# Head outputs of the first branch: transposed by VectorE in 32x32 blocks before they go to DRAM, instead of by TensorE after they come back

## The chip, the cores and the metric

One core of one Trainium2 chip runs the whole kernel. The metric is device time in microseconds of one execution. All times below are from the profile (one execution, with a start and an end for each instruction) or from separate timed runs.

An engine takes its own instructions in order. TensorE is PE in the profile (PEld is its weight load), VectorE is DVE, ScalarE is ACT, GpSimd is POOL, and SyncE is SP. SP issues nearly all transfers on one queue, also in order: an issue that waits for a buffer or for data holds back all issues behind it.

## The reference

The reference is one layer of a hybrid network on 512 tokens of width 1024, in float32: a feed-forward block, a mixing block, a second feed-forward block. The change lies in the mixing block:

```python
z = u @ w_mix + b_mix
q_m, k_m, v_m, o_m, i_m, f_m, q_f, k_f, v_f, f_f, g_a, g_b = split(z)
q_m, k_m = split(silu(causal_conv(concat(q_m, k_m))))
h_m = mlstm_chunkwise(q_m, k_m, v_m, i_m, f_m)            # 4 heads, 256 values each
y_a = sigmoid(o_m) * rms_norm(h_m, mlstm_norm_g).reshape(B, S, 1024)
y_b = forgetting_attention(q_f, k_f, v_f, f_f, ...)       # 16 heads of 64
merged = sigmoid(g_a) * (y_a @ w_branch_a) + sigmoid(g_b) * (y_b @ w_branch_b)
x = x + g2 * (merged @ w_out)
```

`h_m` is the output of the first branch's four heads. It is normalised over each head's 256 values, multiplied by a gate `sigmoid(o_m)`, and then multiplied by `w_branch_a`.

## The kernel before

**Tiling.** 128 partitions (P); the 512 tokens are four blocks of 128 (NT = 4), the width is eight blocks of 128. Each float32 matmul is three passes over parts of the operands: high by high, high by low, low by high (`mm3`, L125 to L129). A weight tile `raw` is loaded by SP, its high part `wh` is made by ScalarE (L102) and its low part `wl` by VectorE (L104). Results go to PSUM banks of two pools: four g banks for the large products, four t banks for the rest. One bank is 128x512.

**The mixing block in order of time.** After the products for the first branch's queries, keys and values (`v_mlstm` makes the values of two heads at a time: bias added by L1037 into `vf`, then `vm` by L1041 and L1042), each of the four heads runs `mlstm_w` (the weights `W`, made from `Mb`, a row of DRAM broadcast to 128 partitions, L1056 to L1078) and `mlstm_h` (the head's output). Between and after these come the second branch's 16 heads: `fox_qkv` (products and normalisation), `fox_s` and `fox_p` (scores, softmax), `fox_o`. The products that do not depend on a head, such as `gate` (tanh of a product into `tg`, then to DRAM as `g_d`) and `y_a`, are generators, and their matmuls are used to fill PE between the heads' steps. The eight `y_a` run between 745 and 820 us, the heads of the first branch end between 480 and 555 us.

**mlstm_h.** Tokens lie on partitions: for each of the four token blocks, matmuls `t<-vm,Wh` give a bank of 128x256 (and two columns for the denominator); L1094 to L1098 divide and write `hn`, one half of a tile of 128x2x256 of tag bc. L1100 sums the squares over the 256 columns (ScalarE). L1103 and `rsqrt` (L146 to L154) make the factors of all four blocks at once, L1106 scales each block in place, and L1107 stores each block (128x256, 128 KB) in a DRAM tensor `h_d` of 512x1024.

**y_a.** Here features lie on partitions, since `y_a` is the moving operand of a later product. For feature block m, eight groups of three matmuls (`gemm_stat`) give `o_m` of 128 features by 512 tokens, L1302 loads the 128 columns of `h_d` as a tile `ht` of 128x4x128 (256 KB, rows of 512 bytes), and four PE transposes (L1305, a matmul with the identity each) put them in a t bank. ScalarE copies the bank into `ya` with a factor (L1307), VectorE multiplies with the gate (L1308).

**What sets the order.** The code is run through a framework that allocates tiles from pools and orders the instructions of each engine itself from program order and its own estimates. A tile has a tag and a tag has a fixed number of buffers; a new tile of the tag waits until the last reader of the oldest is done, and for a tile that is stored this means until the store has landed. The tags that matter: t2 (3 buffers: `hj`, `vf`, `tg`, `th`, `fj`, `vg`, `yt`; `self.tmp` takes one), bc (4 buffers: `hn`, `Mb`, `Mm`, `A`, `Am`), tok (4 buffers: `ht` and token tiles of the second branch).

Of the kernel before, what the change touches and what calls it, by code (L numbers as in the profile page):

```python
# [11 lines left out]
F32 = mybir.dt.float32  # L12
F32R = mybir.dt.float32r
I32 = mybir.dt.int32
AF = mybir.ActivationFunctionType
# [5 lines left out]
P = 128  # L21
T = 512
NT = 4
# [24 lines left out]
class Layer:  # L48
# [1032 lines left out]
    def mlstm_h(self, h, ip):  # L1081
        nc, sp = self.nc, self.sp
        (Wh, Wl), (vh, vl) = self.W[h], self.vt[h]
        ss = sp.tile([P, NT], F32, name=self.nm("hs"), tag="hs", bufs=2)
        hs = []
        for tb in range(NT):
            if tb % 2 == 0:
                h2 = ip.tile([P, 2, 256], F32, name=self.nm("hn"), tag="bc", bufs=4)
            ps = self.tbank()
            for sb in range(tb + 1):  # L1090
                o = W_OFF[sb] + (tb - sb) * P
                self.mm3(ps[:, :258], Wh[:, o:o + P], Wl[:, o:o + P], vh[:, sb, :], vl[:, sb, :], sb == 0, sb == tb)
            d = sp.tile([P, 1], F32, name=self.nm("d"), tag="d", bufs=4)
            nc.vector.tensor_scalar(d, ps[:, 256:257], -1.0, self.gcol[:, tb, 32 + h:33 + h], op0=MUL, op1=MAX)  # L1094
            nc.vector.tensor_tensor(d, d, ps[:, 256:257], op=MAX)
            nc.vector.reciprocal(d, d)
            hn = h2[:, tb % 2, :]
            nc.vector.tensor_scalar(hn, ps[:, 0:256], d, None, op0=MUL)  # L1098
            j = ip.tile([P, 256], F32, name=self.nm("hj"), tag="t2", bufs=3)
            nc.scalar.activation(j, hn, AF.Square, accum_out=ss[:, tb:tb + 1])  # L1100
            hs.append(hn)
        v = sp.tile([P, NT], F32, name=self.nm("hv"), tag="hv", bufs=2)
        nc.vector.tensor_scalar(v, ss, 1.0 / 256, EPS, op0=MUL, op1=ADD)  # L1103
        r = self.rsqrt(v, NT)
        for tb in range(NT):
            nc.vector.tensor_scalar(hs[tb], hs[tb], r[:, tb:tb + 1], None, op0=MUL)  # L1106
            nc.sync.dma_start(self.h_d[tb * P:(tb + 1) * P, h * 256:(h + 1) * 256], hs[tb])  # L1107


    def fox_qkv(self, g, ip):  # L1110
# [176 lines left out]
    def y_a(self, m, ap, ip):  # L1287
        nc = self.nc
        def step():
            if m >= NK // 2:  # L1290
                self.tick()
                next(self.ada)
        ps = self.gbank()
        w = self.w_stat(self.A["w_mix"][0], OM + m * P)
        self.gemm_stat(ps, w, 0, T, range(0, 4))
        step()
        yield
        self.gemm_stat(ps, w, 0, T, range(4, 8))
        th = self.tmp(ip, "th")
        nc.scalar.activation(th, ps, AF.Tanh, scale=0.5, bias=self.hom[:, m:m + 1])  # L1300
        ht = ip.tile([P, NT, P], F32, name=self.nm("ht"), tag="tok", bufs=4)
        nc.sync.dma_start(ht, self.h_d[:, m * P:(m + 1) * P].rearrange("(b p) n -> p b n", p=P))  # L1302
        b = self.tbank()
        for tb in range(NT):
            nc.tensor.transpose(b[:, tb * P:(tb + 1) * P], ht[:, tb, :], self.ident)  # L1305
        ya = ap.tile([P, T], F32, name=self.nm("ya"), tag="qk", bufs=16)
        nc.scalar.activation(ya, b, AF.Copy, scale=self.hmg[:, m:m + 1])  # L1307
        nc.vector.scalar_tensor_tensor(ya, th, 1.0, ya, op0=ADD, op1=MUL)  # L1308
        self.ya[m] = ya
        step()  # L1310
        yield
# [347 lines left out]
```

## Time and profile before

| | us |
|---|---|
| runs, median (lowest to highest of 3) | 1319.72 (1318.76 to 1320.57) |
| profiled execution, its own time | 1320.06 |
| its span (first to last instruction) | 1318.2 |
| PE busy | 1303.2 |
| DVE busy | 955.4 |
| ACT busy | 629.6 |

The span is the time between the first and the last instruction in the trace; the execution's own time has some start and end around it. A row of the timeline gives start, length, engine, line, operation, output and inputs, count, and in brackets the engine's idle time before it and what ended it. Where several equal instructions follow each other, one row shows them with their count, and the length is that of the group. Numbers behind a tile's name are left out in the profile and kept in rows of the order of instructions.

### The profile page before, as it was taken

The numbers are of one execution on the slowest core, as the hardware profiler recorded it, in microseconds if no ns is written. First come the engines' busy times: TensorE is split into PE (matmuls) and PEld (weight loads), VectorE is DVE, ScalarE is ACT, GpSimd is POOL, SyncE is SP. The second block draws the span as 40 slices with busy tenths as digits, with TensorE's granted clock in tenths as the row PEclk, the third lists the DMA queues.
The fourth block names the chain that finished last, engine by engine and source line by source line (L and its number), as shares of the span: only waits on it lengthen the run. The fifth ranks groups of instructions, "written<-read, shape, count | busy, mean of one in ns | idle before, by whom it ended". The sixth has DMA issues, their size and how long they took to land.

```text
span 1318.2 us, 17786 instructions
## 1 busy us (share of the span) xinstructions
PE 1303.2 (99%) x6341; PEld 1092.7 (83%) x6341; DVE 955.4 (72%) x1736; ACT 629.6 (48%) x1054; POOL 36.9 (3%) x57
## 2 busy tenths in 40 slices
PE   7999999999999999999999999999999999999998
PEld 6788888888899888888888888888898888888887
DVE  6887767478688687887887778777567556635787
ACT  5533232355476555566666666334372223223651
POOL 1000000000010101000000000003000000000000
PEclk9999999999999999999999999999999999999999
DMA  9899978465845334533342536777539777634574
GB/s 294 262 326 303 320 268 281 136 193 163 301 126 145 106 111 129 160 104 109 88 129 73 167 105 190 219 251 237 184 104 327 248 238 279 219 100 136 171 263 149
DMA packets 204488, 254.18 MB, mean 193 GB/s; under 512 B 15008, under 2 KB 146752, under 8 KB 204400
## 3 DMA queue, kind: packets, MB, share of 16 engines
q1 hardware_dynamic: 204016, 252.98, 60.4%
q8 instruction: 50, 0.82, 0.3%
q14 instruction: 38, 0.31, 0.1%
q0 software_dynamic: 320, 0.06, 0.0%
q10 hardware_dynamic: 64, 0.02, 0.0%
HBM read 217.28 MB, written 35.72 MB: 192 GB/s over the span
## 4 chain that ended last, share of the span: by engine, by line
PE 93%; DVE 3%; ACT 2%; DMA 1%; issue 1%; ACTq 0%; DVEq 0%
PE g L129 23%; PE g L127 23%; PE g L128 23%; PE t L127 4%; PE t L129 4%; PE t L128 4%; PE g L897 2%; PE t L1280 1%; PE t L1250 1%; PE t L1221 1%; PE t L897 1%; PE t L1222 1%; PE t L797 1%; ACT uh L263 0%; DVE wl L104 0%
## 5 line engine op out<-in xcount | busy, mean ns | idle before, releaser
L102 ACT ACTIVATE wh<-raw 128x1024 fp32r<-128x1024 f32 (+2 forms) x246 | 249.3, 1017 | 373.6 <-PE g L128 128.7
L104 DVE TENSOR_TENSOR wl<-raw,wh 128x1024 fp32r<-128x1024 f32 (+2 forms) x246 | 287.6, 1172 | 160.1 <-ACT wh L102 135.6
L127 PE MATMUL g<-uh,wh 128*128 128x512 f32 (+1 forms) x880 | 341.0, 388 | 0.0
L128 PE MATMUL g<-ul,wh 128*128 128x512 f32 (+1 forms) x880 | 339.5, 386 | 0.4 <-DVE ul L268 0.4
L129 PE MATMUL g<-uh,wl 128*128 128x512 f32 (+1 forms) x880 | 339.6, 386 | 0.0
L129 PEld LDWEIGHTS g<-uh,wl 128*128 128x128 f32 x880 | 165.3, 188 | 33.6
L128 PEld LDWEIGHTS g<-ul,wh 128*128 128x128 f32 x880 | 165.4, 188 | 33.0 <-DVE ul L268 0.6
L127 PEld LDWEIGHTS g<-uh,wh 128*128 128x128 f32 x880 | 165.3, 188 | 32.8 <-issue 0.6
L304 DVE SCALAR_TENSOR_TENSOR acc<-raw,ccol,acc 128x512 f32<-128x512 f32 (+1 forms) x70 | 66.7, 974 | 42.8 <-DMA raw<-in_w_ada_dram 42.7
L127 PE MATMUL g<-wh,uh 128*128 128x512 f32 (+1 forms) x256 | 97.5, 381 | 0.0
L129 PE MATMUL g<-wh,ul 128*128 128x512 f32 (+1 forms) x256 | 96.7, 378 | 0.0
L128 PE MATMUL g<-wl,uh 128*128 128x512 f32 (+1 forms) x256 | 96.4, 377 | 0.0
L127 PE MATMUL t<-wh,A 128*128 128x512 f32 x176 | 68.6, 390 | 0.0
L128 PE MATMUL t<-wl,A 128*128 128x512 f32 x176 | 68.5, 389 | 0.0
L129 PEld LDWEIGHTS g<-wh,ul 128*128 128x128 f32 x256 | 48.2, 188 | 9.0
L127 PEld LDWEIGHTS g<-wh,uh 128*128 128x128 f32 x256 | 48.2, 188 | 8.7 <-DVE tk L1118 0.5
L128 PEld LDWEIGHTS g<-wl,uh 128*128 128x128 f32 x256 | 48.2, 188 | 8.3
L129 PE MATMUL g<-yh,wl 128*128 128x512 f32 x128 | 50.0, 391 | 0.1
L127 PE MATMUL g<-yh,wh 128*128 128x512 f32 x128 | 49.8, 389 | 0.0
L128 PE MATMUL g<-yl,wh 128*128 128x512 f32 x128 | 49.8, 389 | 0.0
L420 ACT ACTIVATE A<-E 128x768 fp32r<-128x768 f32 x22 | 18.6, 846 | 53.4 <-DVE E L419 53.4
L1232 ACT ACTIVATE S<-S,mn 128x128 f32<-128x128 f32 (+1 forms) x64 | 35.5, 556 | 16.1 <-DVE mn L1224 9.9
(353 smaller groups left out, 2242.1 us busy)
## 6 DMA issues: line engine op xcount, KB each, us to landing
raw<-in_ffn_w_in_dram SPq DMA_DIRECT2D x82, 512.0 KB, 4.9
raw<-in_w_ada_dram SPq DMA_DIRECT2D x56, 512.0 KB, 5.7
raw<-in_w_mix_dram SPq DMA_DIRECT2D x46, 512.0 KB, 4.2
sa<-in_ffn_w_out_dram SPq DMA_DIRECT2D x22, 512.0 KB, 5.5
sb<-in_ffn_w_out_dram SPq DMA_DIRECT2D x44, 256.0 KB, 5.2
ws<-sa SPq DMA_DIRECT2D x22, 512.0 KB, 4.6
ws<-sb SPq DMA_DIRECT2D x44, 256.0 KB, 5.0
raw<-ws SPq DMA_DIRECT2D x44, 256.0 KB, 3.5
```

The source lines that it names most:

```text
L102: nc.scalar.activation(hi, src, AF.Copy)
L104: self.last_lo = nc.vector.tensor_tensor(lo, src, hi, op=SUB)
L127: pin(mm(ps, lh, rh, start=start, stop=False))
L128: pin(mm(ps, lh, rl, start=False, stop=False))
L129: self.last_mm = pin(mm(ps, ll, rh, start=False, stop=stop))
L304: nc.vector.scalar_tensor_tensor(a, r[:, s], c, a, op0=MUL, op1=ADD)
L420: nc.scalar.activation(A1[:, 0:3, :], E[:, 0:3, :], AF.Copy)
L797: pin(nc.tensor.transpose(cb[:, 384:512], self.ident, self.ident))
L897: pin(nc.tensor.matmul(acc_ps[b], (wl if p == 1 else wh)[:, b % 2, s], self.ul[k] if p == 2 else self.uh[k], start=k == 0 and p == 0, stop ...
L1221: nc.tensor.matmul(ps[:, :w], q[:, s], k[:, :w], start=True, stop=False)
L1222: nc.tensor.matmul(ps[:, :w], q[:, s], kl[:, :w], start=False, stop=True)
L1232: nc.scalar.activation(S[:, ws], S[:, ws], AF.Exp, scale=-1.0, bias=m, accum_out=sm[:, qb:qb + 1])
```

## The change

Each head's output is now transposed before it is stored. VectorE's transpose works on blocks of 32x32 in place: within each block rows become columns, but the blocks stay where they are. It is done on two token blocks at once (128x512) from `hn` into a new tile `hq` of tag t2, which is stored by one transfer of 256 KB. `h_d` then holds transposed 32x32 blocks at the places of the untransposed ones. In `y_a` the load puts the blocks in place: four loads, each for 32 features, of 32x16x32 (32 partitions, 16 blocks of 32 tokens, rows of 32 values or 128 bytes). The tile `ht` is then 128 features by 512 tokens, the PE transposes and the t bank are left out, and ScalarE copies `ht` to `ya`. The loads now stand ahead of the product in program order, and `ht` is allocated there.

```diff
@@ mlstm_h
-        hs = []
+        hs, h2s = [], []
         for tb in range(NT):
             if tb % 2 == 0:
                 h2 = ip.tile([P, 2, 256], F32, name=self.nm("hn"), tag="bc", bufs=4)
+                h2s.append(h2)
...
         for tb in range(NT):
             nc.vector.tensor_scalar(hs[tb], hs[tb], r[:, tb:tb + 1], None, op0=MUL)
-            nc.sync.dma_start(self.h_d[tb * P:(tb + 1) * P, h * 256:(h + 1) * 256], hs[tb])
+            if tb % 2:
+                t = self.tmp(ip, "hq")
+                nc.vector.transpose(t, h2s[tb // 2].rearrange("p b n -> p (b n)"))
+                nc.sync.dma_start(self.h_d[(tb - 1) * P:(tb + 1) * P, h * 256:(h + 1) * 256].rearrange("(b p) n -> p b n", p=P),
+                                  t.rearrange("p (b n) -> p b n", b=2))
+
+    def blocks(self, t, src):
+
+        for j in range(4):
+            self.nc.sync.dma_start(t[32 * j:32 * j + 32, :].rearrange("a (t b) -> a t b", b=32),
+                                   src[:, 32 * j:32 * j + 32].rearrange("(t a) b -> a t b", a=32))
@@ y_a
         ps = self.gbank()
         w = self.w_stat(self.A["w_mix"][0], OM + m * P)
+        ht = ip.tile([P, T], F32, name=self.nm("ht"), tag="tok", bufs=4)
+        self.blocks(ht, self.h_d[:, m * P:(m + 1) * P])
         self.gemm_stat(ps, w, 0, T, range(0, 4))
...
-        ht = ip.tile([P, NT, P], F32, name=self.nm("ht"), tag="tok", bufs=4)
-        nc.sync.dma_start(ht, self.h_d[:, m * P:(m + 1) * P].rearrange("(b p) n -> p b n", p=P))
-        b = self.tbank()
-        for tb in range(NT):
-            nc.tensor.transpose(b[:, tb * P:(tb + 1) * P], ht[:, tb, :], self.ident)
         ya = ap.tile([P, T], F32, name=self.nm("ya"), tag="qk", bufs=16)
-        nc.scalar.activation(ya, b, AF.Copy, scale=self.hmg[:, m:m + 1])
+        nc.scalar.activation(ya, ht, AF.Copy, scale=self.hmg[:, m:m + 1])
```

The framework then orders some instructions otherwise. Three places follow, each before and with the change. Line numbers behind L1088 are higher in the changed kernel: by 1 up to L1107, by 11 from there to y_a, by 8 behind it.

VectorE at the end of head 0, where the first `vf` of `v_mlstm(1)` is made. Before:

```order
L1098 TENSOR_SCALAR hn_4470<-t_4488,d_4501 128x256
L1037 TENSOR_TENSOR vf_4542<-g_4307,bb_4299 128x512
L1103 TENSOR_SCALAR hv_4508<-hs_4443 128x4
L146 TENSOR_SCALAR rq_4510<-hv_4508 128x4
L148 TENSOR_TENSOR rt_4511<-rq_4510 128x4
L149 SCALAR_TENSOR_TENSOR rd_4513<-rt_4511,hv_4508 128x4
L1042 TENSOR_TENSOR vm_4301<-vf_4542,vm_4301 128x256
```

With the change:

```order
L152 SCALAR_TENSOR_TENSOR rt_4512<-rd_4513 128x4
L153 SCALAR_TENSOR_TENSOR rq_4510<-rt_4511,rq_4510 128x4
L154 SCALAR_TENSOR_TENSOR rq_4510<-rt_4512,rq_4510 128x4
L1107 TENSOR_SCALAR hn_4444<-hn_4444,rq_4510 128x256 x2
L1107 TENSOR_SCALAR hn_4470<-hn_4470,rq_4510 128x256
L1110 STREAM_TRANSPOSE hq_4524<-hn_4444 128x512
L1107 TENSOR_SCALAR hn_4470<-hn_4470,rq_4510 128x256
L1110 STREAM_TRANSPOSE hq_4529<-hn_4470 128x512
L1037 TENSOR_TENSOR vf_4544<-g_4307,bb_4299 128x512
L1095 TENSOR_SCALAR d_4611<-t_4607,gcol 128x1
```

The first `vf` moved from ahead of the whole rsqrt chain to behind the scalings and both transposes. On PE, the first 12 matmuls of the gate that takes this bank moved behind 10 matmuls `t<-vm,Wh` of head 1.

ScalarE between the last `hj` of head 1 and the weights of heads 2 and 3, where that gate's `tg` is made. Before:

```order
L1074 ACTIVATE W_4709<-Mb_4705,gcol 128x384
L1324 ACTIVATE tg_4702<-g_4584,hgg 128x512
L1072 ACTIVATE W_4709<-Mm_4707,gcol 128x128 x2
L1074 ACTIVATE W_4709<-Mb_4705,gcol 128x256
L1072 ACTIVATE W_4709<-Mm_4707,gcol 128x128
L1074 ACTIVATE W_4709<-Mb_4705,gcol 128x128
L1077 ACTIVATE Wh_4710<-W_4709 128x512
```

With the change:

```order
L1074 ACTIVATE W_4713<-Mb_4709,gcol 128x384
L1074 ACTIVATE W_4713<-Mb_4709,gcol 128x256
L1072 ACTIVATE W_4713<-Mm_4711,gcol 128x128 x3
L1074 ACTIVATE W_4713<-Mb_4709,gcol 128x128
L1077 ACTIVATE Wh_4714<-W_4713 128x512
L1072 ACTIVATE W_4713<-Mm_4711,gcol 128x128
L1077 ACTIVATE Wh_4714<-W_4713 128x384
L1074 ACTIVATE W_4829<-Mb_4825,gcol 128x384
L1332 ACTIVATE tg_4706<-g_4586,hgg 128x512
L1072 ACTIVATE W_4829<-Mm_4827,gcol 128x128 x2
```

`tg` moved from behind the first `W<-Mb` of head 2 to behind the first `W<-Mb` of head 3, which waits for the load of `Mb_4825`.

SP at the start of the stretch with y_a. Before:

```order
L1326 DMA g_d_98<-tg_7260 128x512
L1302 DMA ht_7448<-h_d 128x4x128
L1302 DMA ht_7549<-h_d 128x4x128
L1302 DMA ht_7632<-h_d 128x4x128
L1302 DMA ht_7717<-h_d 128x4x128
L92 DMA raw_7776<-in_w_ada_dram 128x1024
L92 DMA raw_7834<-in_w_ada_dram 128x1024
L1326 DMA g_d_99<-tg_7370 128x512
L1210 DMA A_1453_7642<-A_d 128x512
L1302 DMA ht_7824<-h_d 128x4x128
L92 DMA raw_7851<-in_w_mix_dram 128x8x128
```

With the change:

```order
L1334 DMA g_d_98<-tg_7268 128x512
L1117 DMA ht_7418<-h_d 32x16x32 x4
L1117 DMA ht_7499<-h_d 32x16x32 x2
L1334 DMA g_d_99<-tg_7378 128x512
L1117 DMA ht_7499<-h_d 32x16x32 x2
L1117 DMA ht_7582<-h_d 32x16x32 x4
L1221 DMA A_1458_7644<-A_d 128x512
L1117 DMA ht_7681<-h_d 32x16x32 x4
L1117 DMA ht_7762<-h_d 32x16x32 x4
L92 DMA raw_7781<-in_w_ada_dram 128x1024
L1221 DMA A_1489_7785<-A_d 128x512
```

The store of `tg` into `g_d_99` and the first load of `A` now stand among the block loads, and the loads of `in_w_ada` stand behind 20 of them.

## The prediction

> **What bounds the kernel now.** I read the page first, from busy times to the chain of waits, then the chain's engine in stretches of 20 us, then single instructions at the places that the change touches.
>
> ```profile
> span 1318.2 us, 17786 instructions
> PE 1303.2 (99%) x6341; PEld 1092.7 (83%) x6341; DVE 955.4 (72%) x1736; ACT 629.6 (48%) x1054; POOL 36.9 (3%) x57
> PE 93%; DVE 3%; ACT 2%; DMA 1%; issue 1%; ACTq 0%; DVEq 0%
> ```
>
> TensorE is busy for 99% of the span and makes 93% of the chain that ended last. So whatever takes a PE instruction out is worth its pitch on PE, and whatever makes PE wait costs the wait. Work on VectorE, ScalarE and the DMA queue costs nothing until a PE instruction waits for it. Whether it does is a matter of place: the four mLSTM heads end between 480 and 555 us, and y_a runs between 745 and 820. The view by stretches (columns: PE, PEld, DVE, ACT, POOL busy, granted clock, DMA share, GB/s) gives:
>
> ```profile
> 470.00:490.00 20.00, 20.00 (x107) 17.33 (x107) 15.39 (x48) 8.88 (x23) 0.00 (x0) 1.00 0.36 107
> 530.00:550.00 20.00, 19.60 (x108) 16.76 (x107) 18.68 (x68) 12.60 (x26) 0.00 (x0) 1.00 0.51 149
> 550.00:570.00 20.00, 20.00 (x93) 16.61 (x92) 12.64 (x37) 7.97 (x21) 0.00 (x0) 1.00 0.52 150
> 740.00:760.00 20.00, 19.28 (x103) 15.46 (x102) 12.59 (x27) 14.70 (x26) 0.00 (x0) 1.00 0.52 157
> 800.00:820.00 20.00, 20.00 (x110) 17.03 (x109) 17.81 (x28) 12.60 (x22) 0.00 (x0) 1.00 0.63 189
> ```
>
> PE is full in nearly all of them at a granted clock of 1.00. From 530 to 550 VectorE has only 1.3 us of 20 to spare, and PE already loses 0.4 there; from 550 to 570 VectorE has 7.4 us to spare. DMA engines are about half used.
>
> **What is removed: 32 PE transposes, 4 in each of 8 y_a.** They take a bank t and lie in PE's row between gemm matmuls:
>
> ```profile
> 811.39 0.39 PE L128 MATMUL g<-ul,wh 128*128 128x512 f32 x1
> 811.62 0.39 PE L129 MATMUL g<-uh,wl 128*128 128x512 f32 x1
> 811.85 0.60 PE L1305 MATMUL t<-ident,ht 128*128 128x128 f32 x4
> 812.20 0.48 PE L1280 MATMUL t<-Ph,fvt 128*128 128x512 f32 x1
> 812.52 0.39 PE L1280 MATMUL t<-Pl,fvt 128*128 128x512 f32 x1
> L1305 PE MATMUL t<-ident,ht x32: 270/272/273, 761.6 to 819.4; 128*128 128x128 f32 x32
> ```
>
> The last row's 272 ns is the length of one from start to end; matmuls overlap, so the length must not be summed. What counts is the pitch. A 512-column matmul follows the one before by 811.62 − 811.39 = 0.23 us. From the first transpose (811.85) to the second matmul behind the four (812.52) are 0.67 us; without them the same two starts would be 0.23 apart. So four cost 0.67 − 0.23 = **0.44 us**, and the eight y_a 8 × 0.44 = **3.5 us**, 0.27% of the span. The sum by lengths (32 × 0.272 = 8.7 us) would promise more than twice that. The Trainium skill, page "VectorE: DVE Perf Modes", section "The three transpose paths", gives 390 ns for a TensorE transpose of 128x128 in bf16; the trace disagrees for a row of four, with 0.67 − 0.23 over 4, or 0.11 us each.
>
> The copy of the bank to ya on ScalarE stays, now from SBUF: no term.
>
> **What is added on VectorE: 8 transposes of 128x512**, two in each head, on hn before its store. No row shows this operation. The cheapest row of that size is the scaling in the same loop, four of 128x256 in 1.14 us (0.57 for 512 columns); the dearest is a split of twice the columns:
>
> ```profile
> 547.27 1.14 DVE L1106 TENSOR_SCALAR hn<-hn,rq 128x256 f32<-128x256 f32 x4
> 484.58 0.68 DVE L1037 TENSOR_TENSOR vf<-g,bb 128x512 f32<-128x512 f32 x1
> 544.06 1.23 DVE L104 TENSOR_TENSOR wl<-raw,wh 128x1024 fp32r<-128x1024 f32 x1 [0.23 <-ACT wh L102]
> ```
>
> So 0.57 to 1.23 us each; I take **0.75**, just above the 0.68 of an ordinary 128x512 f32 operation (vf). Eight make 6 us of VectorE, 1.5 in a head, and a head's work fits into the idle time that the stretches show, save in 530 to 550. The cost is in who stands behind them. The Trainium skill, same page and section, gives 311 ns for a VectorE transpose of 128x128 in bf16, in 32x32 blocks only; four of these make an estimate of 1.24 us by that page, and with it the sum below would end at 1.8 + 0.9 + 1.8 − 3.5 = +1.0, or 1320.7 us. No row shows which holds.
>
> **What is moved: three places where PE now comes close to a wait.** The tile hq shares the three buffers of tag t2 with vf, tg and others, so each of the next users of the tag waits until a store of hq has landed. One such store of 128 KB landed in 1.8 us, a 256 KB store of tg in 2.5:
>
> ```profile
> DMA to landing us min/median/max: 1.7/1.8/3.4
> g_d<-tg SPq DMA_DIRECT2D x14, 256.0 KB, 2.5
> ```
>
> *Place 1, about 490 us.* The first vf of v_mlstm(1), which frees a g bank, stood ahead of the rsqrt chain of head 0; now it stands behind the chain, four scalings and both transposes. In the trace:
>
> ```profile
> 485.30 0.17 DVE L1103 TENSOR_SCALAR hv<-hs 128x4 f32<-128x4 f32 x1
> 488.32 0.39 PE L127 MATMUL g<-uh,wh 128*128 128x512 f32 x1
> 545.21 0.16 DVE L1103 TENSOR_SCALAR hv<-hs 128x4 f32<-128x4 f32 x1
> 539.25 0.36 PE L127 MATMUL t<-vm,Wh 128*128 128x258 f32 x1 [0.40 <-DVE fq L1200]
> 539.44 0.28 PE L128 MATMUL t<-vm,Wh 128*128 128x258 f32 x1
> 539.56 0.28 PE L129 MATMUL t<-vm,Wl 128*128 128x258 f32 x1
> ```
>
> vf ended at 484.58 + 0.68 = 485.26, and the gate that takes its bank began at 488.32: 3.06 us to spare. Now hv (it needs ScalarE's sum over hj, so still about 485.3), some 1.8 us to the end of the rsqrt (in the last head, hv at 545.21 to scaling at 547.27 is 2.06, with an Am among it), three scalings of 1.14/4, or 0.85, then 0.75, 0.28, 0.75 and vf's 0.6: it ends near 490.3. Twelve of the gate's matmuls have moved behind 10 of t<-vm, whose pitch is 539.56 − 539.44 = 0.12, which gives PE 1.2 us to do meanwhile, up to 488.32 + 1.2 = 489.5. PE waits about **0.8 us** (0.4 at 0.57 us a transpose, 1.8 at 1.23). The next two vf wait for the landings of the hq stores, 2.5 us behind each transpose, near 491.2 and 492.2; vm and the last vf are queued behind them. Their banks are wanted only after the gate's 24 matmuls, 24 × 0.23 = 5.5 us from 490.3, so that costs nothing.
>
> *Place 2, about 506 us.* ScalarE's tg of that gate frees the bank of the fourth fox_qkv(0) gemm. It stood just behind W<-Mb of head 2; now it stands behind W<-Mb of head 3, that is, behind a load that is issued only after a full queue of others:
>
> ```profile
> 493.00 0.46 SPq L1056 DMA_DIRECT2D Mb<-M_d  x1
> 499.09 0.62 ACT L1074 ACTIVATE W<-Mb,gcol 128x384 f32<-128x384 f32 x1 [2.07 <-DMA Mb<-M_d]
> 499.62 0.67 ACT L1324 ACTIVATE tg<-g,hgg 128x512 f32<-128x512 f32 x1
> 503.26 0.32 SPq L1056 DMA_DIRECT2D Mb<-M_d  x1
> 506.45 1.02 ACT L1074 ACTIVATE W<-Mb,gcol 128x384 f32<-128x384 f32 x2 [1.38 <-DMA Mb<-M_d]
> 503.44 0.39 PE L127 MATMUL g<-wh,uh 128*128 128x512 f32 x1
> ```
>
> Before: tg done at 500.3, PE wanted the bank at 503.44. Now Mb of head 3 can be issued at about 502.8 (a buffer of bc and a weight load ahead of it in SP's row); by the second load it lands 3.2 us later (506.45 − 503.26), by the first 6.1 (499.09 − 493.00). tg then ends at about 507.2. PE has nine matmuls of the next chunk moved ahead of the bank's first and comes there at about 506.35. It waits **0.9 us**; with the slow landing 3.7.
>
> *Place 3, about 554 us.* The last head's transposes delay the softmax work of fox_s(0) by 2 to 3 us, and tg of another gate waits for a hq store:
>
> ```profile
> 549.13 0.67 ACT L1324 ACTIVATE tg<-g,hgg 128x512 f32<-128x512 f32 x1
> 553.59 0.39 PE L127 MATMUL g<-wh,uh 128*128 128x512 f32 x1
> ```
>
> tg ended at 549.8, 3.8 us before PE's need. Now the scaling starts near 548.1, the first transpose ends near 549.8, the second near 550.8; its store lands 2.5 later at 553.4, tg ends at 554.2 against PE's 553.4 (after the waits above fall alike on both): **0.8 us**, 1.8 with transposes of 1.23. The softmax itself is not late: PE has other gemms until about 570, in the stretch where VectorE has 7.4 us free.
>
> Sum of waits: 0.8 + 0.9 + 0.8 = **2.5 us**. The upper bound is 1.8 + 3.7 + 1.8 = 7.3. The lower is −0.4: the start times are worked out to within a microsecond, as much as each wait is long, so all may vanish; and hn's buffers of tag bc now come free at the transpose, not when a store has landed, which can release something earlier, but PE's idle time from 470 to 570 is only the 0.40 before the row of 539.25.
>
> **What is added on the queue.** The 16 stores become 8. The 8 loads of ht become 32, of 512 runs of 128 bytes each, and they stand before the gemm. An SP issue of such a form took 2.00/4 = 0.5 us, so 32 take 16 us of SP spread over 45, with the loads of weights and of A behind them. For packets under 512 bytes the stretch of the gate columns' loads is the nearest row:
>
> ```profile
> 375.50 2.00 SPq L92 DMA_DIRECT2D raw<-in_w_mix_dram  x4
> DMA packets 1702, 0.66 MB, mean 164 GB/s; under 512 B 1232, under 2 KB 1573, under 8 KB 1701
> q1 hardware_dynamic: 1701, 0.65, 62.0%
> ```
>
> 62% of 16 engines for 4 us over 1701 packets is 23 ns a packet. One y_a has 2048, which is 2048 × 23/16 = 2.9 us if all engines share; eight make 24 us in 1318, where 8 loads took about 2.8 each. They lie beside PE work. The first A behind them was issued at 759.95 and used at 765.57, 1.8 us after its landing:
>
> ```profile
> 756.20 0.33 SPq L1326 DMA_DIRECT2D g_d<-tg  x1
> 759.95 0.33 SPq L1210 DMA_DIRECT2D A<-A_d  x1
> A<-A_d SPq DMA_DIRECT2D x16, 256.0 KB, 3.8
> 765.57 0.68 DVE L1213 TENSOR_TENSOR Am<-A,maskF 128x512 f32<-128x512 f32 x1
> ```
>
> Six block loads now stand between the g_d store that went out at 756.20 and this A: 756.2 + 0.3 + 6 × 0.5 = 759.5, so A goes out as before. If the 6 × 512 packets ahead of it, 3072 × 23/16 = 4.4 us, are not moved beside its issue, it lands some 4 us late and Am 2 us; even in 800 to 820 VectorE has 2.2 us of 20 to spare. I put no loss here, and C below has the other end. The Trainium skill, page "DMA: Bandwidth & Descriptors", section "Specifications", says line rate needs 512 bytes and that below it the engine does read-modify-write, a rule against this change; the 23 ns above, with 72% of packets below that size, do not show it.
>
> **Sum.** The profiled execution took 1320.06 us (span 1318.2 and 1.9 around it), 0.34 above the median of the runs. 1320.06 − 3.5 + 2.5 = 1319.06, on the median's scale 1319.72 − 1.0 = 1318.7. I forecast **1318.7 us**: most of the gain is given back. 0.2% (2.6 us) is about what a measurement of this kernel can tell from no change: faster is below 1317.1, slower above 1322.4.
>
> **Rivals.** A: *all waits are covered.* If hv starts earlier, Mb lands early or the waits fall on each other (a PE wait at place 1 gives places 2 and 3 the same time), 3.5 us are gained: 1316.2 us. For it: each wait is under 1 us; against it: three places at once. B: *tag t2 and the Mb load hold PE.* Waits at their upper bounds, 7.3 us: 1319.7 − 3.5 + 7.3 = 1323.5, slower. It decides once the waits exceed 3.5 + 2.6 = 6.1 us. For it: the 6.1 us of the first Mb; against it: the second took 3.2 with the same queue. C: *the block loads hold SP's queue and the DMA engines between 745 and 820.* A load of 64 KB on 32 partitions may use few engines: on four, a y_a's 2048 packets take 2048 × 23/4 = 11.8 us, longer than the 8 us from y_a to y_a (761.6 to 819.4 over 7); then ya is late by 3.5 us each, on all but the first four buffers, and weights queue behind: 4 × 3.5 − 3.5 = 10.5 us slower, 1330. Against it: the four loads of one y_a go to different partitions. D: *the change removes nothing from the path*, since the fox loop in y_a's stretch waits for VectorE (17.81 of 20 busy there): 1319.7 + 2.5 = 1322.2. Against it: PE is at 20.00 there.
>
> **Chances.** Forecast 0.43 (its own range 1317.0 to 1320.7), A 0.24, B 0.15, C 0.10, D 0.08. Faster by over 0.2%: A and a little of the forecast, 0.28. Slower: B, C and a little of D, 0.28. The rest, 0.44, is within it. The range leaves 0.1 above, most of C, and under 0.1 below: 1315.8 (A with the run-to-run spread) to 1323.5 (B).
>
> **What would show it.** Right: no L1305, and L1280 follows a gemm matmul at 0.23; PE waits near 490, 506 and 554, each near 1 us, for vf, tg and tg; a transpose near 0.75. Wrong: a transpose above 1 us or below 0.6; block loads that land in over 6 us or PE below 20.00 from 760 to 820; waits at places not named, above all in 530 to 550, where VectorE has least to spare.

## The result: slower by 0.7%

| | us |
|---|---|
| before, median of 6 runs (lowest to highest) | 1319.92 (1318.76 to 1320.57) |
| with the change, median of 6 | 1329.39 (1327.99 to 1331.16) |
| ratio, 95% interval | 1.0073 (1.0063 to 1.0084) |

The time lies 6 us above the upper end of the predicted range. The profiled execution is the fastest of the six, with a span of 1326.1 us, 7.9 more than before; the medians lie 9.5 apart, and the other 1.6 us are not in this trace. First the page: span, busy times and the chain of waits.

```profile
span 1326.1 us, 17750 instructions
PE 1303.3 (98%) x6309; PEld 1090.1 (82%) x6309; DVE 959.5 (72%) x1744; ACT 630.9 (48%) x1054; POOL 36.6 (3%) x57
PE 87%; DVE 6%; ACT 2%; DMA 2%; issue 1%; SPq 1%; POOL 0%; DVEq 0%; ACTq 0%
```

PE has 32 instructions fewer, as intended, and is as long busy as before, so some of the others took longer. Its share of the chain fell from 93% to 87%, and DVE's rose from 3% to 6%. The view of PE alone shows where it stood still (idle time ahead of a row is in brackets; waits that the kernel before has too are left out). The last four rows have no wait and show the pitch:

```profile
489.46 0.50 PE L127 MATMUL g<-uh,wh 128*128 128x512 f32 x1 [0.32 <-DVE vf L1037]
507.12 0.50 PE L127 MATMUL g<-wh,uh 128*128 128x512 f32 x1 [1.42 <-ACT tg L1332]
556.01 0.50 PE L127 MATMUL g<-wh,uh 128*128 128x512 f32 x1 [0.41 <-ACT tg L1332]
...
813.58 0.50 PE L127 MATMUL g<-uh,wh 128*128 128x512 f32 x1 [0.46 <-ACT wh L102]
815.16 0.50 PE L129 MATMUL g<-uh,wl 128*128 128x512 f32 x1 [0.85 <-DVE wl L104]
824.61 0.79 PE L127 MATMUL g<-uh,wh 128*128 128x512 f32 x1 [4.15 <-ACT wh L102]
826.22 0.80 PE L129 MATMUL g<-uh,wl 128*128 128x512 f32 x1 [0.40 <-DVE wl L104]
827.24 0.63 PE L128 MATMUL g<-ul,wh 128*128 128x512 f32 x1
827.67 0.63 PE L129 MATMUL g<-uh,wl 128*128 128x512 f32 x1
829.72 0.40 PE L128 MATMUL g<-ul,wh 128*128 128x512 f32 x1
829.95 0.40 PE L129 MATMUL g<-uh,wl 128*128 128x512 f32 x1
```

The first three are the places 1 to 3 of the prediction. The next four were not foreseen: 0.46 + 0.85 + 4.15 + 0.40 = 5.9 us of waiting for the split weights of the last y_a and of the first gate behind it. Behind the longest, matmuls follow each other at 827.67 − 827.24 = 0.43 us instead of 829.95 − 829.72 = 0.23. The view by stretches says why: the granted clock (the third column from the end) is 0.83 there, while the stall of 1.42 us near 507 left it at 1.00.

```profile
500.00:520.00 20.00, 18.58 (x86) 15.23 (x85) 13.20 (x32) 11.28 (x26) 3.93 (x4) 1.00 0.41 129
800.00:820.00 20.00, 18.70 (x96) 15.47 (x95) 14.66 (x23) 8.71 (x15) 0.00 (x0) 1.00 0.68 185
820.00:840.00 20.00, 15.45 (x58) 11.80 (x58) 18.72 (x27) 12.66 (x19) 0.00 (x0) 0.83 0.63 186
```

From 826.22 to 829.72 are 8 matmuls in 3.50 us that take 8 × 0.23 = 1.84 at full clock; with the first two after the stall that is some 2.4 us more.

The account: waits in the heads 0.32 + 1.42 + 0.41, less the 0.40 near 539 that is gone, 1.8 us (a row of VectorE splits weights at 744.62 before and at 747.13 now, so 2.5 us had been lost by then); PE transposes −3.5; late stalls 5.9; lower clock 2.4. Sum 1.8 + 5.9 + 2.4 − 3.5 = 6.6 of the 7.9 us, and with the 2.5 instead of the 1.8, 7.3. A wait of 0.49 us at 894.87, shown below, is in neither sum. The expected gain did come, and was given back three times over.

### The profile page after: what moved, and what is told of

Read it like the earlier page. It is cut to its first block, busy times and chain, and to the rows that moved or that the text cites. A ratio compares the mean times of both kernels' runs of the same rounds, so it can differ in the third digit from the quotient of the medians.

```text
span 1326.1 us, 17750 instructions
## 1 busy us (share of the span) xinstructions
PE 1303.3 (98%) x6309; PEld 1090.1 (82%) x6309; DVE 959.5 (72%) x1744; ACT 630.9 (48%) x1054; POOL 36.6 (3%) x57
## 4 chain that ended last, share of the span: by engine, by line
PE 87%; DVE 6%; ACT 2%; DMA 2%; issue 1%; SPq 1%; POOL 0%; DVEq 0%; ACTq 0%
PE g L129 22%; PE g L127 22%; PE g L128 22%; PE t L127 4%; PE t L129 4%; PE t L128 4%; PE g L897 1%; PE t L1291 1%; PE t L1261 1%; DVE wl L104 1%; PE t L1232 1%; PE t L1233 1%; PE t L897 1%; SPq L808 1%; DMA ar<-in_w_ada_dram 1%
```

## The experiments

All ratios are to the kernel before, run on the same chip in the same rounds. Two theories about two places: Q, that the block loads in SP's queue make the weights late; T, that hq in tag t2 is what the heads pay for.

**One half at a time.** e1 takes the heads of the change and y_a of the kernel before; e2 the reverse.

```diff
e1, y_a:
-        ht = ip.tile([P, T], F32, ...); self.blocks(ht, ...)
+        ht = ip.tile([P, NT, P], F32, ...); one load; four PE transposes
e2, mlstm_h:
-            if tb % 2: t = self.tmp(ip, "hq"); nc.vector.transpose(t, ...); one store of two blocks
+            nc.sync.dma_start(self.h_d[tb * P:(tb + 1) * P, h * 256:(h + 1) * 256], hs[tb])
```

> Heads as in the changed kernel (VectorE transposes, hq stores); y_a as before, with one load and four PE transposes, so that ya holds wrongly placed values. Theory Q (the block loads in SP's queue cost most): only the three waits of the heads are left, 0.3 near 490, 1.4 between 500 and 520, 0.6 between 540 and 560, in all 2.4 us: 1319.9 + 2.4 = 1322.3. Rival H (the heads' transposes and stores, which shift everything behind them, cause the late stall too): 1329 or more, as the 3.5 us of PE transposes are back.

> Heads as before (stores of hn, no VectorE transposes); y_a as in the changed kernel, so that ya holds blocks that are not transposed. Theory Q: the stalls near 814 and 825 stay, with the lower clock behind the second; 1329.4 - 2.4 = 1327. Rival H: the stalls are gone, 1319.9 - 3.5 = 1316.4.

Measured: e1 1.0031 (1.0021 to 1.0042), +4.1 us; e2 1.0038 (1.0024 to 1.0051), +5.0 us. Together 9.1, close to the change's 9.5: the halves add. The late stalls and the lower clock of the change are 5.9 + 2.4 = 8.3 us, and 8.3 − 3.5 = 4.8 is what e2 costs, to 0.2. e2 has the stalls at 811.68, 813.27 and 822.71 with the same lengths (0.46, 0.86, 4.15) and the clock of 0.83 behind them, and in the heads only 0.41 at 539.96, which the kernel before has too; so H falls and the late stalls belong to the loads. e1 cost 1.7 us more than Q expected. Its rows of PE:

```profile
490.42 0.50 PE L127 MATMUL g<-uh,wh 128*128 128x512 f32 x1 [0.33 <-DVE vf L1037]
508.35 0.50 PE L127 MATMUL g<-wh,uh 128*128 128x512 f32 x1 [1.70 <-ACT tg L1335]
885.08 0.50 PE L129 MATMUL g<-yh,wl 128*128 128x512 f32 x1 [1.23 <-DVE wl L104]
```

Beside the waits of places 1 and 2 (place 3 has none here) there is 1.23 us near 885, at a weight split for the branch products, where the kernel before has 0.15 from 880 to 900:

```profile
894.87 0.50 PE L129 MATMUL g<-yh,wl 128*128 128x512 f32 x1 [0.49 <-DVE wl L104]
```

This is the change's own row near that place. e5 has 0.53 there, e10 0.55, e8 0.28, and e2, e3, e4, e6, e7, e9 and e11 have no such wait. That it comes from work shifted by some 2 us is an inference; no run was made for it. The waits of e1, less the 0.40 and the 0.15 of the kernel before, make 2.7 of its 4.1 us; the rest is not traced.

**The loads: who issues them, how many, how wide.**

```diff
e3, blocks:
-            self.nc.sync.dma_start(t[32 * j:32 * j + 32, :]...
+            self.nc.gpsimd.dma_start(t[32 * j:32 * j + 32, :]...
e4, y_a:
-        self.blocks(ht, self.h_d[:, m * P:(m + 1) * P])
+        nc.sync.dma_start(ht.rearrange("p (b n) -> p b n", b=NT), self.h_d[:, m * P:(m + 1) * P].rearrange("(b p) n -> p b n", p=P))
e8, y_a:
-        self.blocks(ht, self.h_d[:, m * P:(m + 1) * P])
+        four loads as in e4, of 32 partitions each
```

> The changed kernel with the 32 block loads issued by POOL instead of SP; the packets stay. Theory Q: loads of weights go out as early as before, no stall at 814 and 825: 1319.9 - 3.5 + 2.4 = 1318.8, and wl of the fourth weight tile of y_a is again near 773. Rival P (the 128-byte packets fill the DMA engines and the weights land late, whoever issues them): stalls stay, 1326 to 1329.

> The changed kernel with one load of 512-byte rows into ht for each y_a, at the new place ahead of the product, instead of four of 128-byte rows; ya then holds wrongly placed values. Theory Q: 8 issues instead of 32, stalls gone, 1318.8. Rival P: also gone. Rival O (what costs is that the loads stand ahead of the product and the tile ht is held longer, so that the order of the rest is worse): stalls stay, 1326 or more.

> The changed kernel with the four loads of a y_a made of 512-byte rows (32 partitions by 4 token blocks by 128 values), so that ya holds wrongly placed values: as many SP issues and bytes as the change, a quarter of the packets. Theory C (the count of issues in SP's queue costs): stalls stay, 1327 or more. Rival K (it is the 128-byte rows, by their own time or by the order that the framework makes for them): as with one load, 1321.

Measured: e3 1.0006 (0.9996 to 1.0017); e4 1.0000 (0.9991 to 1.0009); e8 0.9988 (0.9978 to 0.9998). In none of the three does PE wait between 800 and 835. So the transfers' own time is not the cause (e3 has the same 128-byte rows), nor their place ahead of the product (e4), nor their number in SP's queue (e8 has 32). Of the theories, C (of e8's expectation, not the prediction's rival C), O and P fall, and Q's count of loads in SP's queue with them; e8's K is left, and as e3 has the rows on POOL without a stall, what remains is that 128-byte rows *on SP* give a bad order.

e8 and the change can be compared row by row, as both issue 32 loads on SP. SP and ScalarE of e8, the first weight load behind the first two loads of in_w_ada, and its split:

```profile
766.78 0.91 SPq L92 DMA_DIRECT2D raw<-in_w_ada_dram  x2
774.05 0.40 SPq L92 DMA_DIRECT2D raw<-in_w_mix_dram  x1
779.01 1.06 ACT L102 ACTIVATE wh<-raw 128x1024 fp32r<-128x1024 f32 x1 [2.41 <-DMA raw<-in_w_mix_dram]
```

The same in the change, where ScalarE's row of th ahead of it is shown too:

```profile
768.38 0.49 SPq L92 DMA_DIRECT2D raw<-in_w_ada_dram  x1
771.37 0.38 SPq L92 DMA_DIRECT2D raw<-in_w_mix_dram  x1
788.18 0.69 ACT L1313 ACTIVATE th<-g,hom 128x512 f32<-128x512 f32 x1 [1.27 <-PE g L129]
789.98 1.08 ACT L102 ACTIVATE wh<-raw 128x1024 fp32r<-128x1024 f32 x1
```

The change issues this weight load 2.7 us *earlier* than e8, and splits it 11 us later. In e8, wh waits for the transfer (the bracket). In the change it does not; it stands in ScalarE's order behind the th of two more y_a than in e8 (those of 780.10 and 788.18), and th waits for PE. Nothing was late on SP or on the DMA engines here.

From there the delay runs in a circle. raw has three buffers, and two loads of in_w_ada go between two weight loads, so each weight load takes the buffer of the one before and is issued when that one's wl is done. VectorE, SP and ScalarE of the change:

```profile
793.97 1.22 DVE L104 TENSOR_TENSOR wl<-raw,wh 128x1024 fp32r<-128x1024 f32 x1
795.22 0.38 SPq L92 DMA_DIRECT2D raw<-in_w_mix_dram  x1
...
803.74 1.21 DVE L104 TENSOR_TENSOR wl<-raw,wh 128x1024 fp32r<-128x1024 f32 x1
804.98 0.38 SPq L92 DMA_DIRECT2D raw<-in_w_mix_dram  x1
...
812.48 1.05 ACT L102 ACTIVATE wh<-raw 128x1024 fp32r<-128x1024 f32 x1
813.89 1.22 DVE L104 TENSOR_TENSOR wl<-raw,wh 128x1024 fp32r<-128x1024 f32 x1
815.13 0.38 SPq L92 DMA_DIRECT2D raw<-in_w_mix_dram  x1
...
820.49 0.69 ACT L1313 ACTIVATE th<-g,hom 128x512 f32<-128x512 f32 x1 [5.60 <-PE g L129]
...
823.51 1.04 ACT L102 ACTIVATE wh<-raw 128x1024 fp32r<-128x1024 f32 x1
```

Each load goes out within 0.03 us of the end of a wl (795.19, 804.95, 815.11). For the load of 815.13 alone, the view of L92 gives the time from issue to landing:

```profile
DMA to landing us min/median/max: 4.8/4.8/4.8
```

The loads are 10 us apart, and a y_a takes PE about 8. The load issued at 815.13 had landed at 819.9. Its wh starts at 823.51, 3.6 us after that, behind th of the last y_a and three yh. PE needs it at 820.46 (824.61 − 4.15). So 3.6 of the 4.15 us are wh's place in the order; with wh at once behind the landing (819.9 + 1.04) PE would have waited about 0.5, an estimate. The kernel before, ScalarE at the same two weights:

```profile
804.54 1.06 ACT L102 ACTIVATE wh<-raw 128x1024 fp32r<-128x1024 f32 x1 [2.70 <-DMA raw<-in_w_mix_dram]
811.11 1.06 ACT L102 ACTIVATE wh<-raw 128x1024 fp32r<-128x1024 f32 x1 [1.13 <-DMA raw<-in_w_mix_dram]
```

There the two wh stand ahead of the th of 805.50 and 813.37, two y_a earlier in the order than in the change, wait for their transfers, and start when these land: 6.6 us from one to the next.

**Moving the weights forward, with the block loads left on SP.** e7 makes the weights of the next y_a (and of the first gate) one step earlier in program order, e9 two steps; th is queued behind the wh of those weights. e11 moves the block loads behind the product instead.

```diff
e9, y_a (e7: one weight instead of two in the list):
+        ws = self.wq = self.wq if m else [self.w_stat(..., OM + k * P) for k in range(2)]
-        w = self.w_stat(self.A["w_mix"][0], OM + m * P)
+        w = ws.pop(0)
...
+        ws.append(self.w_stat(..., OM + (m + 2) * P if m < NK - 2 else GA + (m + 2 - NK) * P))
         self.gemm_stat(ps, w, 0, T, range(4, 8))
         th = self.tmp(ip, "th")
+        with self.tc.issue_after(self.last_wh.ins):
             nc.scalar.activation(th, ps, AF.Tanh, ...)
e11, y_a:
-        ht = ...; self.blocks(...)          # ahead of gemm_stat
+        ht = ...; self.blocks(...)          # behind th
```

> The changed kernel, block loads on SP as they are; only the weights of the next y_a (and of the first gate behind y_a) are taken one step earlier in program order, and ScalarE's th of a y_a is queued behind the split wh of those weights. Theory S (the weights have landed in time, and PE waits because wh stands behind th on ScalarE, so that load, split and load again of the one weight buffer make a circle longer than a y_a): the stalls near 814 and 825 shrink to under 1 us, no lower clock, 1329.4 - 7 = 1322.4. Rival L (the weights land too late, as SP issues the blocks ahead of them): stalls of 5 us or more stay, 1328 or more.

> The changed kernel with its block loads on SP; the weights of y_a (and of the two gates behind) are now taken two steps earlier in program order, and th is queued behind the split wh of those. In SP's order one weight load moves ahead of eight block loads, and on ScalarE each wh ahead of one more th. Theory S (the place of wh and of the weight loads in the order, set one y_a too late, is the cause, and neither the count of issues nor the 128-byte rows): no stall of over 1 us between 800 and 835, 1321.5 + 0.6 = 1322 as with POOL's loads (heads 4.1, gain 3.5). Rival L (with the blocks on SP the weights can't be had in time): 1326 as in the run with the weights one step earlier, or more.

> The changed kernel with the block loads (and the tile ht) behind the product in program order, where the one load stood before. If their place ahead of the product causes the stalls: as the kernel before plus 0.6. By theory S the order of wh against th is what counts, and that is the same here as in the change: stalls stay, ratio 1.005 or more.

Measured: e7 1.0030 (1.0020 to 1.0040); e9 1.0034 (1.0020 to 1.0048); e11 1.0062 (1.0047 to 1.0077). e11 is as S expected: with the loads behind the product there is still a stall of 5.28 us. e7 costs 4.0 us where the change costs 9.5; S's 1322.4 is 1.0019, just under its interval, and L's 1328 is 1.0061, far above. Of the change's two places the last y_a has no wait left and the first gate 0.33 + 0.53 us, and the granted clock stays at 1.00. But PE waits now for weights behind these, which e7 did not move: 0.41 + 0.53 us at the second gate, and 1.77 at a branch weight, where it is the transfer that comes late:

```profile
829.07 0.38 SPq L92 DMA_DIRECT2D raw<-in_w_branch_a_dram  x1
834.16 1.06 ACT L102 ACTIVATE wh<-raw 128x1024 fp32r<-128x1024 f32 x1 [3.05 <-DMA raw<-in_w_branch_a_dram]
835.26 0.50 PE L127 MATMUL g<-yh,wh 128*128 128x512 f32 x1 [1.77 <-ACT wh L102]
```

e9 misses S's number: 1322 would be 1.0016, below its interval, while L's 1326 is 1.0046, inside it. Its trace shows why. SP, ScalarE and PE in order of time:

```profile
823.69 0.38 SPq L92 DMA_DIRECT2D raw<-in_w_branch_a_dram  x1
...
831.05 2.18 ACT L1360 ACTIVATE yh<-ya 128x512 fp32r<-128x512 f32 x4
833.13 1.99 ACT L102 ACTIVATE wh<-raw 128x1024 fp32r<-128x1024 f32 x2
...
834.23 0.79 PE L127 MATMUL g<-yh,wh 128*128 128x512 f32 x1 [3.80 <-ACT wh L102]
```

Between 800 and 830 no stall is left: the weights that were moved come in time, with all 32 block loads on SP, so L falls for them, whatever the time. But the next weight in the stream, the first of w_branch_a, was not moved. It goes out at 823.69, where the kernel before issues it at 818.62, and its wh stands behind a row of yh. With the 3.6 us to landing that the loads of that stretch have, it had landed near 827.3 (an estimate), 5.8 us ahead of its wh. PE stalls 3.80 us there, and the clock is 0.83 again. The stall has changed places, not gone: S names the mechanism, and the edit mends it for the weights that it moves. e7 and e9 move a weight's load and its wh together, so no run separates the two; it is the rows at 815.13 and 823.51 above that give most of the change's stall to wh. The loads of in_w_ada, which take the other two buffers, were not moved.

**The heads, and both repairs.** e5 gives hq a buffer of tag p6 (five buffers, used by W, Wh, Wl) instead of t2; e6 adds POOL's issues of e3 to that, e10 the weights of e9.

```diff
-                t = self.tmp(ip, "hq")
+                t = ip.tile([P, 1280], F32, name=self.nm("hq"), tag="p6", bufs=5)[:, 0:512]
```

> The changed kernel with hq in the five buffers of tag p6 (W, Wh, Wl of the heads) instead of t2; nothing else is edited, and vf and tg are back at their old places in the order. Theory T (the heads' 4.1 us come from hq in t2, which moves vf and tg behind the transposes and behind Mb of head 3): the waits near 490 and 507 go, 1329.4 - 4 = 1325.4. Rival V (VectorE's 5.6 us of transposes are what the heads pay): 1329, the waits only move.

> hq in tag p6 and the block loads on POOL: both repairs at once. If both theories hold, the 3.5 us of PE transposes are left as a gain: 1320.5 - 3.5 = 1317.0 on the scale of the kernel before. If they hide one another or POOL's loads make waits of their own in the fox loop: 1320 or more.

> The same with hq in tag p6: all on SP, both repairs. Theory S and T together: ratio to the kernel before near 1 - 3.5/1320 = 0.9973, as with POOL's loads. If the repairs work only apart: 1.000 or more.

Measured: e5 1.0036 (1.0025 to 1.0046); e6 **0.9963 (0.9949 to 0.9977)**, 1318.0 against 1322.0 us in the same rounds; e10 1.0010 (1.0000 to 1.0019). In e5, vf and tg are back at their old places in the order, PE waits neither near 490 nor near 507, and the change's +9.5 has become +4.8: T holds, V falls, as the eight transposes are all still there. e5 keeps the late stalls (0.46, 0.85, 4.15 as in the change, and 0.89 for 0.40). e6 has neither. Its page:

```profile
span 1316.6 us, 17784 instructions
PE 1300.3 (99%) x6309; PEld 1088.8 (83%) x6309; DVE 957.4 (73%) x1744; ACT 630.5 (48%) x1054; POOL 57.1 (4%) x89
```

PE is busy for 2.9 us less than before and still 99%; POOL's 32 issues cost it 20 us of an engine that is idle otherwise. This version is faster than both kernels, and its interval holds the 0.27% that the PE transposes are worth. e10 misses its 0.9973: it keeps e9's stall of 3.80 us at the first branch weight, and so the gain is lost.

## Why the prediction was wrong

- **The removed transposes, 0.44 us each, 3.5 in all: right.** Between 747 and 808 the change makes up 2.7 us on the kernel before over six y_a (weights split 2.51 us later at 747.13, the row of ten PE transposes at 807.82 instead of 807.99), 0.45 each; in that stretch PE has 334 matmuls before and 310 now, 24 fewer, which are just these transposes. e6 is 3.0 to 6.7 us faster by its interval, which holds the whole 3.5.
- **The cost of a VectorE transpose, 0.75 taken, 0.57 to 1.23 as bounds: right.** The row of the group, with the least, median and greatest length in ns:

```profile
L1110 DVE STREAM_TRANSPOSE hq<-hn x8: 700/702/712, 487.1 to 552.8; 128x512 f32<-128x512 f32 x8
```

  The estimate of 1.24 us from the Trainium skill, page "VectorE: DVE Perf Modes", section "The three transpose paths", falls: four 128x128 pieces in one instruction cost 0.70.
- **The three waits in the heads: right in place and releaser, and near in the sum.** Place 1: 0.32 for 0.8, since hv began at 484.75 and not at 485.3. Place 2: 1.42 for 0.9: tg ended at 507.06, as worked out (507.2), but PE, less held at place 1, came at 505.70 and not at 506.35; in e1, e3, e4, e7, e8, e9 and e11 it is 1.6 to 1.9. Place 3: 0.41 for 0.8; that tg waited there for the landing of a hq store is not shown, as ScalarE is busy with the softmax up to tg's start at 555.30. Sum 2.15 for 2.5. The heads alone (e1) cost 4.1, so this term was too small; e1's wait of 1.23 us near 885 is the part of the difference that has a place.
- **"What is added on the queue … I put no loss here": this step failed.** It followed one load behind the blocks, A, and no PE wait came from A. It named the loads of weights as standing behind the blocks, and then put them at nothing without a price. And it asked for lateness on SP and the DMA engines only. The runs showed that at the longest stall the transfer came within about half a us of the need, and that the static order of ScalarE (wh behind th and yh) and the three raw buffers made a circle of 10 us against 8 us of PE work: 5.9 us of stalls and 2.4 of lower clock where the sum has 0. The order of wh and th on ScalarE is not among the prediction's three places. With e1's 4.1 for the heads and 8.3 for this term the prediction's own sum gives 1319.9 − 3.5 + 4.1 + 8.3 = 1328.8, against 1329.4 measured.
- **The rivals.** C had the stretch, the sign and, at 1330, nearly the time, but the time by luck, as the mechanism was another: it had the block loads themselves too slow, for which ya would wait. A load landed in 3.5 us in the median, and ya waited for none of them. A chance of 0.10 for it and an end of the range at B's 1323.5 were too little for a queue whose largest users had not been followed. B's 7.3 us in the heads did not come; D falls with e6, where the removed transposes are a gain. A's 1316.2, 3.5 us under the kernel before, needed both e5's and e3's edits (e6).

What stays open: why the framework gave 128-byte rows on SP this order. Its own estimates are not on record. That it takes such rows for slower than they are is an inference from e3, e4 and e8; measured, a block load lands in 3.5 us, and in 2.0 with the wide rows of e8.

## What to carry to other kernels

When a change adds transfers to a queue, price the largest stream behind them, not the nearest: follow each of its loads through buffer, split and consumer, and see whether one more place back in the order closes a circle through a small pool. Read the order of the engine that turns a load into something usable (here ScalarE's wh), since a load that has landed is worth nothing behind an instruction that waits for PE. A temporary that is stored should not share a small pool with tiles that release PSUM banks; here another tag took back half of the loss (e5), a second queue nearly all of it (e3, 1.0006), and the two together left the gain (e6).

## What the runs showed of the hardware

A long stall of PE cost more than its length here. After 4.15 us of idling (820.46 to 824.61), matmuls of 512 columns ran at a pitch of 0.43 us until 829.4. In all six kernels with a stall of 3.8 to 5.3 us between 800 and 840 (the change, e2, e5, e9, e10, e11) the granted clock fell, to 0.83 or 0.91 from 820 to 840; the 5.6 us ahead of the change's first matmul show 1.00. The Trainium skill, page "TensorE: Matmul & The Clock Gate", section "Part 1: The HAM clock gate (the "warmup" mystery)", says that after an idle window of about 3.4 us the clock is halved until a busy window of that length has passed; the trace agrees in the halving, but the clock fell before PE had been idle for that long. In stretches of 2 us, the change:

```profile
820.00:822.00 2.00, 0.45 (x2) 0.03 (x1) 0.79 (x2) 0.75 (x2) 0.00 (x0) 1.00 0.32 129
822.00:824.00 2.00, 0.00 (x0) 0.00 (x0) 2.00 (x4) 2.00 (x4) 0.00 (x0) 0.69 0.00 0
824.00:826.00 2.00, 1.22 (x2) 0.50 (x2) 2.00 (x3) 1.95 (x4) 0.00 (x0) 0.50 0.79 189
```

A mean of 0.69 from 822 to 824 puts the fall from 1.00 to 0.50 near 822.8, which is 2.3 us after PE stopped. In e5, whose stall is as long (818.13 to 822.28), the same working on 0.84 from 822 to 824 puts it near 823.4, when PE had started again. So the length of a stall does not fix the moment. For shorter stalls it does not even fix whether the clock falls. In e3 and e4 PE waited 1.93 us for the same tg. The rows of e3:

```profile
510.72 0.50 PE L127 MATMUL g<-wh,uh 128*128 128x512 f32 x1 [1.93 <-ACT tg L1332]
...
512.62 0.63 PE L128 MATMUL g<-wl,uh 128*128 128x512 f32 x1
513.04 0.63 PE L129 MATMUL g<-wh,ul 128*128 128x512 f32 x1
```

and of e4:

```profile
507.59 0.50 PE L127 MATMUL g<-wh,uh 128*128 128x512 f32 x1 [1.93 <-ACT tg L1332]
507.93 0.40 PE L128 MATMUL g<-wl,uh 128*128 128x512 f32 x1
508.17 0.39 PE L129 MATMUL g<-wh,ul 128*128 128x512 f32 x1
```

In e3's profiled execution the clock fell 1.5 us after the stall, for 3.4 us (pitch 0.42); in e4's, after the same stall, it did not. e3 shows it a second time, where a wait of 1.94 us ends at 12.99 and the granted clock from 14 to 16 is 0.50. So a stall of under 2 us was followed by a loss of 1.6 us more in one execution (eight matmuls at 0.43 for 0.23) and by none in another, which may be part of why e3's ten runs go from 1320.55 to 1325.75.
